# Weights as differences of suffix products, and a softmax divided at the gates

## The chip, the cores and the metric

One Trainium2 chip, one of its cores. The metric is the device time of one execution of the whole program, in microseconds (us). A core has five engines with queues of their own, which run in order: PE (matmul and transposes), DVE (vector), ACT (activation functions and copies), POOL (general vector work) and SP, which here issues every DMA.

## The reference, cut to what matters

One layer is run on a prompt of 1024 tokens and on a sample of 32 tokens with caches of 512. From one input projection come queries, keys, values and gates for two groups of eight heads of width 64. The A heads are a softmax over a band of 64-token chunks with a bias by clipped distance. The B heads are stick-breaking attention: a key's weight is its own sigmoid times the product of the complements of all later keys. Both outputs are multiplied with a SiLU of their gates.

```python
def band_attention(q, k, v, q_pos, k_pos, bias_table):
    s = jnp.einsum('bqhd,bkhd->bhqk', q, k).astype(jnp.float32) * ATTN_SCALE
    rel = jnp.clip(k_pos[None, :] - q_pos[:, None], -REL_CLIP, REL_CLIP) + REL_CLIP
    s = s + bias_table[:, rel].astype(jnp.float32)[None]
    ...
    w = jax.nn.softmax(s, axis=-1).astype(v.dtype)
    return jnp.einsum('bhqk,bkhd->bqhd', w, v)

def stick_breaking(q, k, v, q_pos, k_pos):
    z = jnp.einsum('bqhd,bkhd->bhqk', q, k).astype(jnp.float32) * ATTN_SCALE
    causal = (k_pos[None, :] < q_pos[:, None])[None, None]
    log_beta = jax.nn.log_sigmoid(z)
    log_1m = jnp.where(causal, jax.nn.log_sigmoid(-z), 0.0)
    after = lax.cumsum(log_1m, axis=3, reverse=True) - log_1m
    w = jnp.where(causal, jnp.exp(log_beta + after), 0.0).astype(v.dtype)
    return jnp.einsum('bhqk,bkhd->bqhd', w, v)

def finish(h, oa, ga, ob, gb, w_out, g_post, p, w_ple, w_ple_gate):
    y = jnp.concatenate([oa * jax.nn.silu(ga), ob * jax.nn.silu(gb)], axis=-1) @ w_out
    h = h + rmsnorm(y, g_post)
    return h + jax.nn.sigmoid(h @ w_ple_gate) * (p @ w_ple)
```

## The kernel before, in words

**Who sets the order.** The program is not issued as it is written. Every operation is recorded (`Recorder.add`) with its engine, its operands and what it must follow. `Recorder.order` then runs a list scheduling over all recorded operations, with a cost for each form (`Recorder.cost`), 60 ns per semaphore, 400 ns of margin ahead of PE and 2 us behind a DMA. On PE, class 0 (attention) goes ahead of class 1 (projections) whenever both are ready. `emit` issues the result, so nearly all instructions carry its line, L450, and are told apart by their tiles. The order on each engine is fixed by then; on the chip an engine only waits.

**Numbers.** Matmuls split an operand into a rounded high part and a rest (`kdA` and `klA`, `wTh` and `wTl`, `hnh` and `hnl`), so a product takes two or three matmuls.

**The stages.** After an opening (norm of the input, first projections, part of the per-layer embedding), eight pairs of heads follow in the order A0, B0, A1, B1 up to A3, B3. While the heads of one pair are computed, `weave` lays in the projections `q`, `k`, `v` of the next (`col_steps`, tiles `mm_qA` and so on, 3 chunks of 352 columns, 24 matmuls each). With the last pair, B3, come the eight gate projections, `gA` of four pairs and then `gB`. The two output products follow, as a seven-product scheme over four row blocks (`o0P` to `g3P`), and a tail.

**One head** (`attention`) has eight row blocks of 128 queries. `scores` computes a block: two matmuls for a piece of up to 512 keys into a PSUM bank of tag `S` (three of them). Blocks of more than 512 keys are done as two pieces. Working tiles come from two rings, `om` (w0) and `be` (w1, 3384 columns).

- *A* adds the bias and takes the running maximum in one DVE operation (`om<-SA,biasA`, tile `statA` for the maximum); DVE negates the maximum, ACT takes the exponential with the sum of the row, DVE the reciprocal, and POOL scales the block:

```python
                nc.vector.tensor_scalar(m[:, 2:3], m[:, last:last + 1], -1.0, None, ALU.mult)
                nc.scalar.activation(w1[:, 0:n], w0[:, 0:n], AF.Exp, bias=m[:, 2:3], accum_out=m[:, 3:4])
                nc.vector.reciprocal(m[:, 3:4], m[:, 3:4])
                nc.gpsimd.tensor_scalar(w1[:, 0:n], w1[:, 0:n], m[:, 3:4], 1.0, ALU.mult, ALU.mult)
```

- *B* adds a mask on the diagonal (DVE), takes sigmoid(-z) into w0 and sigmoid(z) into w1 (ACT), runs a product from the last key backwards over w0, shifted by one slot (DVE scan, with a column of ones that POOL sets at the end), and POOL multiplies w1 with it.

`weights_t` turns a block: PE transposes four 128x128 squares into a bank of tag `T` (two of them, `ptwA`, `ptwB`), ACT copies it to `wTh`, DVE subtracts to get `wTl`. Blocks 4 and 6 of A go by a transpose on DVE and a swap through DRAM instead. `values` multiplies with the values (`PVA`, `PVB`), and the head's output goes to DRAM (`o_dr`).

**At the gates** (`mms` in `col_steps`, `k == "g"`) ACT takes the sigmoid of a chunk (`sggA`, three buffers), DVE multiplies it with the chunk, which frees the PSUM bank, POOL multiplies with the head outputs loaded back from `o_dr` (`oggA`, tag `bias`, two buffers), and the result goes to `og_dr`, from where the output products read it.

**The sample's heads** (`sample_attention`) come beside pairs A1, B1, A3 and B3 and divide their own softmax. Their output fills columns 1024 to 1055 of `o_dr`. The tag `stg` (three buffers) holds the projected `st` tiles of q, k and v, and after the gates the split inputs of the per-layer embedding (`php`) and rows of the output products.

Of the kernel before, what the change touches and what calls it, by code (L numbers as in the profile page):

```python
# [455 lines left out]
def stream_step(  # L456
# [19 lines left out]
    def scratch(shape, name):  # L476
        return Buf(shape, F32, name=name, real=dram.tile(shape, F32, tag=name, name=name))

    o_dr = [scratch([P, T], f"o_dr{n}") for n in range(8)]
    og_dr = scratch([8, P, T], "og_dr")  # L480
    h1_dr = scratch([T, D], "h1_dr")
    sum_dr = {w: scratch([4, 4, P, 512], f"sum_dr{w}") for w in "og"}
# [28 lines left out]
    at0 = rec.pool(ctx, tc, name="at0", bufs=1)  # L511
    at = rec.pool(at_stack, tc, name="at", bufs=1)
    opnd = [at0, at]
    ring0, ring1 = Arena(rec, at, "om", 3076), Arena(rec, at, "be", 3384)
    ringh, ringl = (Arena(rec, at, x, 33 * P, F32R) for x in ("wTh", "wTl"))

    def rstd_of(ms, name, n):
# [6 lines left out]


    NAMES = ["qA", "kA", "vA", "gA", "qB", "kB", "vB", "gB"]

    raws, loaded = {}, {}

# [76 lines left out]
    def bias_rows():  # L606

        rb = ring0.tile([8, 257], "rb")
        dma(rb, rel_bias[0])
        R = ring1.tile([8, 768], "R")  # L610
        nc.gpsimd.memset(R, 0.0)
        nc.vector.tensor_scalar(R[:, 256:768], R[:, 256:768], rb[:, 0:1], None, ALU.add)
        nc.vector.tensor_copy(R[:, 0:256], rb[:, 0:256][:, ::-1])
        dma(r_dr, R)

    def bias_src(h, rows, first, cols):
# [95 lines left out]
    def col_steps(j):  # L712

        kind, p = order[j]
        ab, k = kind[1], kind[0]
        n = sidx(ab, p)
        box = {}
        steps = []

        def mms(c, part):  # L720
            if part == 0:
                if c == 0:
                    ensure(j)
                    ensure(j + 1)
                    if k != "g":
                        box["st"] = at2.tile([P, T], F32, tag="stg", name=f"st{kind}{p}", bufs=3)
                box["acc"] = psum("mm", f"mm_{kind}{p}_{c}")[:, 0:CH]
            acc = box["acc"]
            cs = slice(c * CH, (c + 1) * CH)
            if k == "g" and part == 0:  # L730
                box["og"] = at2.tile([P, CH], F32, tag="bias", name=f"og{kind}{p}_{c}", bufs=2)
                dma(box["og"], o_dr[n][:, cs])
            W = loaded[j]
            for x in range(part * 24 // PARTS, (part + 1) * 24 // PARTS):
                q, k8 = x // KD, x % KD
                a = W[k8 // 4][1 if q == 1 else 0]
                b = (hnl if q == 2 else hnh)[c]
                nc.tensor.matmul(acc, a[:, k8 % 4, :], b[:, k8, :], start=(x == 0), stop=(x == 23))
            if part < PARTS - 1:
                return  # L740
            if k == "g":
                sg = at2.tile([P, 512], F32, tag="sg", name=f"sg{kind}{p}_{c}", bufs=3)[:, 0:CH]
                nc.scalar.activation(sg, acc, AF.Sigmoid)
                nc.vector.tensor_tensor(sg, acc, sg, ALU.mult)
                nc.gpsimd.tensor_tensor(sg, sg, box["og"], ALU.mult)
                dma(og_dr[n, :, cs], sg)
            elif k == "q":
                nc.scalar.activation(box["st"][:, cs], acc, AF.Copy, scale=SCALE)
            else:
                nc.scalar.copy(box["st"][:, cs], acc)  # L750

        for c in range(NCH):
            for part in range(PARTS):
                steps.append((3.6 / PARTS, lambda c=c, part=part: mms(c, part), GATE_NEEDS.get((kind, p)) if part == 0 else None))

        def after_q():
            src_of["q", ab, p] = box["st"]
            nc.gpsimd.tensor_scalar(qsS[:, slot(ab, p), :], box["st"][:, SEQ:T], 1.0, 1.0, ALU.mult, ALU.mult)

        def after_k():  # L760
            src_of["k", ab, p] = box["st"]
            nc.gpsimd.tensor_scalar(ksS[:, slot(ab, p), :], box["st"][:, SEQ:T], 1.0, 1.0, ALU.mult, ALU.mult)

        def after_v(tok):
            src_of["v", ab, p] = tok
            dma(vs_dr[ab][:, p * P:(p + 1) * P], tok[0:NS, 8, :])

        if k == "q":
            steps.append((0.0, after_q))
        elif k == "k":  # L770
            steps.append((0.0, after_k))
            steps += keys_out(ab, p, lambda: box["st"], *((ak_p, ak_s) if ab == "A" else (bk_p, bk_s)))
        elif k == "v":
            steps += values_out(ab, p, lambda: box["st"], *((av_p, av_s) if ab == "A" else (bv_p, bv_s)), after_v)
        return steps


    def attention(ab, p, h):
# [5 lines left out]
        def begin():  # L784
            if ab == "A":
                bias = at2.tile([P, 640], F32, tag="bias", name=f"bias{nm}", bufs=2)
                dma(bias, bias_src(2 * p + h, P, 0, 640))
                nc.gpsimd.memset(bias[0:HD, 0:HD], NEG)
                nc.gpsimd.memset(bias[HD:P, 576:640], NEG)
                box["bias"] = bias  # L790

        def lo_block(i):
            return max(0, i - 4) if ab == "A" else 0
# [19 lines left out]
        def scores(i):  # L813
            L, kd, kl = Lq[h], KDh[h], KLD[h]
            b0 = lo_block(i)
            n = (i + 1 - b0) * P
            k0 = b0 * P
            cut = [0, n] if n <= 512 else [0, n // 2, n]
            w0, w1 = rooms(i)
            pieces = []  # L820
            for j in range(len(cut) - 1):
                s = psum("S", f"S{nm}_{i}_{j}")[:, 0:cut[j + 1] - cut[j]]
                lhs = L[:, i * P:(i + 1) * P]
                ks = slice(k0 + cut[j], k0 + cut[j + 1])
                nc.tensor.matmul(s, lhs, kd[:, ks], start=True, stop=False)
                nc.tensor.matmul(s, lhs, kl[:, ks], start=False, stop=True)
                pieces.append((cut[j], cut[j + 1], s))
            if ab == "B":
                a, b, s = pieces[-1]
                dg = s[:, b - a - P:b - a]  # L830
                nc.vector.tensor_tensor(dg, dg, maskb, ALU.add)
                nc.gpsimd.memset(w0[:, n:n + 1], 1.0)
                for a, b, s in pieces:
                    nc.scalar.activation(w0[:, a:b], s, AF.Sigmoid, scale=-1.0)
                for a, b, s in pieces:
                    nc.scalar.activation(w1[:, a:b], s, AF.Sigmoid)
                for a, b, s in reversed(pieces):
                    rev = w0[:, a + 1:b + 1][:, ::-1]
                    nc.vector.tensor_tensor_scan(rev, rev, s, 1.0 if b == n else w0[:, b + 1:b + 2], ALU.mult, ALU.bypass)
                nc.gpsimd.tensor_tensor(w1[:, 0:n], w1[:, 0:n], w0[:, 1:n + 1], ALU.mult)  # L840
            else:
                m = small.tile([P, 4], F32, tag="stat", name=f"stat{nm}_{i}", bufs=6)
                for j, (a, b, s) in enumerate(pieces):
                    nc.vector.tensor_tensor_reduce(
                        w0[:, a:b], s, box["bias"][:, n - b:n - a][:, ::-1], 1.0,
                        -3e38 if j == 0 else m[:, j - 1:j], ALU.add, ALU.max, m[:, j:j + 1])
                last = len(pieces) - 1
                nc.vector.tensor_scalar(m[:, 2:3], m[:, last:last + 1], -1.0, None, ALU.mult)
                nc.scalar.activation(w1[:, 0:n], w0[:, 0:n], AF.Exp, bias=m[:, 2:3], accum_out=m[:, 3:4])
                nc.vector.reciprocal(m[:, 3:4], m[:, 3:4])  # L850
                nc.gpsimd.tensor_scalar(w1[:, 0:n], w1[:, 0:n], m[:, 3:4], 1.0, ALU.mult, ALU.mult)
            state[i] = w0, w1

        wT = {}
# [92 lines left out]
    def sample_attention(ab, gi):  # L947
# [44 lines left out]
        def scores():  # L992
# [20 lines left out]
            else:  # L1013
                m = small.tile([P, 4], F32, tag="stat", name="stat" + nm, bufs=6)
                for j, (a0, b0, s) in enumerate(pieces):
                    nc.vector.tensor_tensor_reduce(
                        w0[:, a0:b0], s, bx["bias"][:, NK - b0:NK - a0][:, ::-1], 1.0,
                        -3e38 if j == 0 else m[:, 0:1], ALU.add, ALU.max, m[:, j:j + 1])
                nc.vector.tensor_scalar(m[:, 2:3], m[:, 1:2], -1.0, None, ALU.mult)
                nc.scalar.activation(w1[:, 0:NK], w0[:, 0:NK], AF.Exp, bias=m[:, 2:3], accum_out=m[:, 3:4])  # L1020
# [360 lines left out]
    for x in ple.later:  # L1381
        dma(*x)
        rec.behind()
    bias_rows()
    for h in range(4):
        dma(masks[h * NS:(h + 1) * NS, :], maskb[0:NS, 0:NS])
    for j in range(3):
# [463 lines left out]
```

## Time and profile before

| | us |
|---|---|
| median of 3 runs | 806.25 (804.82 to 810.35) |
| span of the profiled execution | 802.6 |
| PE busy | 792.0 |
| DVE, ACT, POOL busy | 565.7, 539.5, 469.5 |
| mean granted TensorE clock | 0.999 |

The profile is one execution, from its first to its last instruction, 802.6 us; the runs' times are 2.2 to 7.8 us longer than that span. A group of the profile has its engine, operation, tiles and shapes; then the time in which at least one of its instructions ran and the mean ns of one (instructions overlap, so the mean times the count can be more), then the engine's idle time ahead of them and what ended it. In a timeline, a row has its start, the time until its end, and how many instructions it merges; the difference of two starts on PE is the step at which instructions follow each other. A wait is put down to the engine whose signal came last.

### The profile page before, as it was taken

Reading aid. Unit: us, or ns where it says so; the run is one execution under the profiler, and the core shown is the slowest. Engines: PE = TensorE matmul, PEld = TensorE weight load, DVE = VectorE, ACT = ScalarE, POOL = GpSimd, SP = SyncE. Lnnn points to the kernel's source line nnn. Section 1 sums busy time; section 2 is a strip of 40 time slices with the busy share of each in tenths; the row PEclk is TensorE's granted clock in tenths of the full one; section 3 lists DMA queues with packets and bytes.
Section 4 is the critical chain, followed back from the end, with each engine's and each line's share of the span. In section 5 each row is a group of like instructions: output and inputs, shape, how many; then the busy total and the mean of one; then the engine's idle time right before and its main releaser. Section 6 shows DMA issues by size and latency. Waiting matters only on the chain.

```text
span 802.6 us, 14554 instructions
## 1 busy us (share of the span) xinstructions
PE 792.0 (99%) x4734; PEld 731.4 (91%) x4734; DVE 565.7 (70%) x1129; ACT 539.5 (67%) x1163; POOL 469.5 (58%) x554
## 2 busy tenths in 40 slices
PE   9999999999999999999999999999999999999997
PEld 7899999999999999999999899999998877888786
DVE  7627878777787888776787586854554786587655
ACT  6636787786586777776787577644437868876741
POOL 6625867795686866635473265554553448599613
PEclk9999999999999999999999999999999999999999
DMA  9419986538876565833325656344389957769634
GB/s 293 135 46 285 236 230 186 153 112 254 220 229 198 145 184 158 208 103 102 92 60 141 146 158 205 99 149 138 105 277 300 288 174 242 236 197 345 215 117 131
DMA packets 147390, 146.32 MB, mean 182 GB/s; under 512 B 37409, under 2 KB 109257, under 8 KB 147314
## 3 DMA queue, kind: packets, MB, share of 16 engines
q1 hardware_dynamic: 147314, 145.39, 61.3%
q8 instruction: 38, 0.62, 0.3%
q14 instruction: 38, 0.31, 0.1%
HBM read 90.78 MB, written 46.16 MB: 171 GB/s over the span
## 4 chain that ended last, share of the span: by engine, by line
PE 89%; DVE 3%; DMA 2%; POOL 2%; ACT 1%; issue 1%; SPq 1%; POOLq 0%; DVEq 0%; ACTq 0%
PE mm_gB L450 6%; PE mm_gA L450 6%; PE mm_kB L450 6%; PE mm_qB L450 6%; PE mm_qA L450 5%; PE mm_kA L450 5%; PE mm_vB L450 4%; PE PVB L450 4%; PE mm_vA L450 4%; PE SB L450 4%; PE ptwB L450 4%; PE SA L450 3%; PE PVA L450 3%; PE g0P L450 2%; PE g1P L450 2%; PE o1P L450 2%
## 5 line engine op out<-in xcount | busy, mean ns | idle before, releaser
L450 POOL TENSOR_TENSOR be<-be,om 128x512 f32<-128x512 f32 (+8 forms) x66 | 82.9, 1260 | 77.8 <-DVE om L450 43.9
L450 DVE TENSOR_TENSOR_SCAN om<-om,SB 128x384 f32<-128x384 f32 (+5 forms) x96 | 92.6, 968 | 21.9 <-ACT be L450 11.7
L450 POOL TENSOR_SCALAR be<-be,statA 128x640 f32<-128x640 f32 (+3 forms) x64 | 44.4, 698 | 44.4 <-DVE statA L450 35.8
L450 DVE TENSOR_TENSOR wTl<-ptwB,wTh 128x512 fp32r<-128x512 f32 (+3 forms) x96 | 50.8, 546 | 13.8 <-ACT wTh L450 12.4
L450 ACT ACTIVATE om<-SB 128x384 f32<-128x384 f32 (+5 forms) x96 | 47.4, 499 | 19.0 <-DVE SB L450 14.2
L450 ACT CAST wTh<-ptwB 128x512 fp32r<-128x512 f32 (+3 forms) x96 | 44.6, 483 | 14.5 <-PE ptwB L450 10.5
L450 ACT ACTIVATE be<-om,statA 128x640 f32<-128x640 f32 (+3 forms) x64 | 44.6, 698 | 11.2 <-DVE statA L450 9.6
L450 ACT ACTIVATE be<-SB 128x384 f32<-128x384 f32 (+5 forms) x96 | 46.8, 498 | 6.8 <-DVE om L450 6.3
L450 PE MATMUL ptwB<-ident,be 128*128 128x128 f32 x288 | 44.0, 273 | 0.1
L450 PEld LDWEIGHTS ptwB<-ident,be 128*128 128x128 f32 x288 | 34.9, 140 | 2.2 <-PE mm_vA L450 0.4
L450 DVE CUSTOM_DVE_ANT_0 om<-SA,biasA 128x320 f32<-128x320 f32 (+2 forms) x64 | 30.7, 480 | 5.3 <-PE SA L450 4.9
L450 PE MATMUL SB<-kdB,LB 128*128 128x384 f32 (+5 forms) x96 | 34.0, 357 | 0.3 <-DVE om L450 0.3
L450 ACT CAST wTh<-ptwA 128x512 fp32r<-128x512 f32 (+2 forms) x64 | 26.0, 429 | 12.0 <-PE ptwA L450 11.4
L450 DVE TENSOR_TENSOR wTl<-ptwA,wTh 128x512 fp32r<-128x512 f32 (+2 forms) x64 | 29.7, 482 | 4.9 <-ACT wTh L450 4.0
L450 PE MATMUL SB<-klB,LB 128*128 128x384 f32 (+5 forms) x96 | 32.9, 347 | 0.0
L450 PE MATMUL SA<-kdA,LA 128*128 128x320 f32 (+2 forms) x96 | 30.0, 319 | 1.1 <-DVE LA L450 0.8
L450 PE MATMUL SA<-klA,LA 128*128 128x320 f32 (+2 forms) x96 | 29.8, 319 | 0.0
L450 POOL TENSOR_TENSOR gB<-gB,gB 128x256 f32<-128x256 f32 x32 | 26.6, 848 | 0.7 <-DMA gB<-in_w_ple_gate_dram 0.4
L450 PE MATMUL ptwA<-ident,be 128*128 128x128 f32 x160 | 26.5, 274 | 0.0
L450 DVE TENSOR_TENSOR SB<-SB,maskb 128x128 f32<-128x128 f32 x64 | 18.0, 292 | 9.9 <-PE SB L450 8.0
L450 POOL TENSOR_TENSOR oB<-oB,oB 128x256 f32<-128x256 f32 x32 | 23.6, 754 | 1.4 <-DMA oB<-in_w_out_dram 1.3
L450 POOL TENSOR_TENSOR h<-h,x 128x512 f32<-128x512 f32 (+1 forms) x18 | 23.0, 1295 | 0.8 <-DVE h L450 0.8
(706 smaller groups left out, 2668.3 us busy)
## 6 DMA issues: line engine op xcount, KB each, us to landing
swapA<-om SPq DMA_DIRECT2D x16, 320.0 KB, 3.5
be<-swapA SPq DMA_DIRECT2D x64, 80.0 KB, 2.9
oB<-in_w_out_dram SPq DMA_DIRECT2D x16, 256.0 KB, 3.9
sum_dro<-oB SPq DMA_DIRECT2D x16, 256.0 KB, 2.9
gB<-in_w_ple_gate_dram SPq DMA_DIRECT2D x16, 256.0 KB, 3.7
sum_drg<-gB SPq DMA_DIRECT2D x16, 256.0 KB, 3.2
x<-in_x_prompt_dram SPq DMA_DIRECT2D x16, 256.0 KB, 4.1
h_dr<-h SPq DMA_DIRECT2D x8, 512.0 KB, 3.6
```

The costliest lines, as they stand in the source:

```text
L450: getattr(getattr(tc.nc, o.what[0]), o.what[1])(*args, **kw)
```

## The change

*B.* The second sigmoid goes. The scan runs over w0 in place and unshifted, from the column of ones at its end, so that w0 holds the products of the complements from each key on; a weight is the difference of two neighbours, which POOL takes in place of its product.

*A.* Queries are scaled by -1/8 and the bias rows are negated, so the DVE operation takes a minimum of the negated scores, and ACT's exponential (scale -1) uses it directly as its bias. Weights are left undivided. The row sums of a head's eight blocks gather in one 128x8 tile (`sums`); after the eighth, DVE takes reciprocals, PE turns them (`pts`), ACT copies them out and a DMA stores eight rows of 128 in `rs_dr` in DRAM. At the gates of A, two DMAs per chunk spread the rows of the two heads over 64 partitions each, and POOL multiplies once more. Columns of the sample in `rs_dr` are ones. The loaded tiles at the gates have two halves and come from tag `stg`. Ring `be` has 3328 columns.

```diff
-    ring0, ring1 = Arena(rec, at, "om", 3076), Arena(rec, at, "be", 3384)
+    ring0, ring1 = Arena(rec, at, "om", 3076), Arena(rec, at, "be", 3328)
...
+    def fixed_columns():
+        x = small.tile([8, NS], F32, tag="fixed", name="fixed")
+        nc.gpsimd.memset(x, 1.0)
+        dma(rs_dr[:, SEQ:T], x)
...
-        nc.vector.tensor_scalar(R[:, 256:768], R[:, 256:768], rb[:, 0:1], None, ALU.add)
-        nc.vector.tensor_copy(R[:, 0:256], rb[:, 0:256][:, ::-1])
+        nc.vector.tensor_scalar(R[:, 256:768], R[:, 256:768], rb[:, 0:1], None, ALU.subtract)
+        nc.vector.tensor_scalar(R[:, 0:256], rb[:, 0:256][:, ::-1], -1.0, None, ALU.mult)
...
-                box["og"] = at2.tile([P, CH], F32, tag="bias", name=f"og{kind}{p}_{c}", bufs=2)
-                dma(box["og"], o_dr[n][:, cs])
+                box["og"] = at2.tile([P, 2, CH], F32, tag="stg", name=f"og{kind}{p}_{c}", bufs=3)
+                dma(box["og"][:, 0], o_dr[n][:, cs])
+                if ab == "A":
+                    for h in range(2):
+                        row = rs_dr.real[2 * p + h:2 * p + h + 1, cs]
+                        dma(box["og"][h * HD:(h + 1) * HD, 1], Raw(rs_dr, bass.AP(tensor=row.tensor, offset=row.offset, ap=[[0, HD], [1, CH]])))
...
-                nc.gpsimd.tensor_tensor(sg, sg, box["og"], ALU.mult)
+                nc.gpsimd.tensor_tensor(sg, sg, box["og"][:, 0], ALU.mult)
+                if ab == "A":
+                    nc.gpsimd.tensor_tensor(sg, sg, box["og"][:, 1], ALU.mult)
...
-                nc.scalar.activation(box["st"][:, cs], acc, AF.Copy, scale=SCALE)
+                nc.scalar.activation(box["st"][:, cs], acc, AF.Copy, scale=-SCALE if ab == "A" else SCALE)
...
-                for a, b, s in pieces:
-                    nc.scalar.activation(w1[:, a:b], s, AF.Sigmoid)
                 for a, b, s in reversed(pieces):
-                    rev = w0[:, a + 1:b + 1][:, ::-1]
-                    nc.vector.tensor_tensor_scan(rev, rev, s, 1.0 if b == n else w0[:, b + 1:b + 2], ALU.mult, ALU.bypass)
-                nc.gpsimd.tensor_tensor(w1[:, 0:n], w1[:, 0:n], w0[:, 1:n + 1], ALU.mult)
+                    rev = w0[:, a:b][:, ::-1]
+                    nc.vector.tensor_tensor_scan(rev, rev, s, w0[:, b:b + 1], ALU.mult, ALU.bypass)
+                nc.gpsimd.tensor_tensor(w1[:, 0:n], w0[:, 1:n + 1], w0[:, 0:n], ALU.subtract)
...
-                        -3e38 if j == 0 else m[:, j - 1:j], ALU.add, ALU.max, m[:, j:j + 1])
+                        3e38 if j == 0 else m[:, j - 1:j], ALU.add, ALU.min, m[:, j:j + 1])
                 last = len(pieces) - 1
-                nc.vector.tensor_scalar(m[:, 2:3], m[:, last:last + 1], -1.0, None, ALU.mult)
-                nc.scalar.activation(w1[:, 0:n], w0[:, 0:n], AF.Exp, bias=m[:, 2:3], accum_out=m[:, 3:4])
-                nc.vector.reciprocal(m[:, 3:4], m[:, 3:4])
-                nc.gpsimd.tensor_scalar(w1[:, 0:n], w1[:, 0:n], m[:, 3:4], 1.0, ALU.mult, ALU.mult)
+                nc.scalar.activation(w1[:, 0:n], w0[:, 0:n], AF.Exp, bias=m[:, last:last + 1], scale=-1.0, accum_out=sums[:, i:i + 1])
+                if i == 7:
+                    nc.vector.reciprocal(sums, sums)
+                    pt = psum("T", f"pts{nm}")
+                    nc.tensor.transpose(pt[0:8, 0:P], sums, ident)
+                    row = at.tile([P, 4 * P], F32, tag="ot", name=f"sumrow{nm}", bufs=2)[0:8, 0:P]
+                    nc.scalar.copy(row, pt[0:8, 0:P])
+                    dma(rs_dr[2 * p + h, 0:SEQ].rearrange("(i q) -> i q", q=P), row)
```

The sample's A heads change only by the sign: minimum for maximum, and no negation. In the bias tiles the masked corners become +1e30.

More of the change, by code (lines that the diff above doesn't have):

```diff
@@ L479, in stream_step @@
     o_dr = [scratch([P, T], f"o_dr{n}") for n in range(8)]
+    rs_dr = scratch([8, T], "rs_dr")
     og_dr = scratch([8, P, T], "og_dr")
@@ L787, in begin @@
                 dma(bias, bias_src(2 * p + h, P, 0, 640))
-                nc.gpsimd.memset(bias[0:HD, 0:HD], NEG)
-                nc.gpsimd.memset(bias[HD:P, 576:640], NEG)
+                nc.gpsimd.memset(bias[0:HD, 0:HD], -NEG)
+                nc.gpsimd.memset(bias[HD:P, 576:640], -NEG)
                 box["bias"] = bias
+                box["sums"] = small.tile([P, 8], F32, tag="sums", name=f"sums{nm}", bufs=2)
         def lo_block(i):
@@ L834, in scores @@
                     nc.scalar.activation(w0[:, a:b], s, AF.Sigmoid, scale=-1.0)
-                for a, b, s in pieces:
-                    nc.scalar.activation(w1[:, a:b], s, AF.Sigmoid)
                 for a, b, s in reversed(pieces):
-                    rev = w0[:, a + 1:b + 1][:, ::-1]
-                    nc.vector.tensor_tensor_scan(rev, rev, s, 1.0 if b == n else w0[:, b + 1:b + 2], ALU.mult, ALU.bypass)
-                nc.gpsimd.tensor_tensor(w1[:, 0:n], w1[:, 0:n], w0[:, 1:n + 1], ALU.mult)
+                    rev = w0[:, a:b][:, ::-1]
+                    nc.vector.tensor_tensor_scan(rev, rev, s, w0[:, b:b + 1], ALU.mult, ALU.bypass)
+                nc.gpsimd.tensor_tensor(w1[:, 0:n], w0[:, 1:n + 1], w0[:, 0:n], ALU.subtract)
             else:
                 m = small.tile([P, 4], F32, tag="stat", name=f"stat{nm}_{i}", bufs=6)
+                sums = box["sums"]
                 for j, (a, b, s) in enumerate(pieces):
@@ L1017, in scores @@
                         w0[:, a0:b0], s, bx["bias"][:, NK - b0:NK - a0][:, ::-1], 1.0,
-                        -3e38 if j == 0 else m[:, 0:1], ALU.add, ALU.max, m[:, j:j + 1])
-                nc.vector.tensor_scalar(m[:, 2:3], m[:, 1:2], -1.0, None, ALU.mult)
-                nc.scalar.activation(w1[:, 0:NK], w0[:, 0:NK], AF.Exp, bias=m[:, 2:3], accum_out=m[:, 3:4])
+                        3e38 if j == 0 else m[:, 0:1], ALU.add, ALU.min, m[:, j:j + 1])
+                nc.scalar.activation(w1[:, 0:NK], w0[:, 0:NK], AF.Exp, bias=m[:, 1:2], scale=-1.0, accum_out=m[:, 3:4])
                 nc.vector.reciprocal(m[:, 3:4], m[:, 3:4])
@@ L1384, in stream_step @@
     bias_rows()
+    fixed_columns()
     for h in range(4):
```

## The prediction

> **What bounds the kernel now.** I read the page's busy times first, then a table of stages, then who made PE wait, then single stretches of PE's timeline. The page, with its span and its engines:
>
> ```profile
> span 802.6 us, 14554 instructions
> PE 792.0 (99%) x4734; PEld 731.4 (91%) x4734; DVE 565.7 (70%) x1129; ACT 539.5 (67%) x1163; POOL 469.5 (58%) x554
> ```
>
> PE is busy for 792.0 of 802.6 us. The other engines have room on average, but an average hides stages, so the next view cuts the span into the opening, the attention heads, the gates with the last head, the two final products and the tail. Its columns are PE, weight loads, DVE, ACT, POOL, granted clock, DMA share and GB/s.
>
> ```profile
> 0.00:40.00 40.00, 36.97 (x210) 32.79 (x211) 28.38 (x44) 25.26 (x49) 24.51 (x46) 1.00 0.68 215
> 40.00:480.00 440.00, 437.59 (x2840) 422.44 (x2839) 330.94 (x751) 314.28 (x695) 266.03 (x332) 1.00 0.60 166
> 480.00:600.00 120.00, 120.00 (x773) 117.61 (x772) 73.55 (x124) 63.33 (x145) 66.61 (x70) 1.00 0.52 160
> 600.00:780.00 180.00, 180.00 (x831) 144.01 (x830) 121.74 (x193) 132.79 (x268) 105.86 (x102) 1.00 0.73 238
> 780.00:802.60 22.60, 17.49 (x88) 14.56 (x86) 11.14 (x19) 3.79 (x7) 6.45 (x5) 0.98 0.36 117
> ```
>
> PE's idle time is 3.03 us in the opening, 5.11 us in the tail, and 440 - 437.59 = 2.41 us in all the attention between them; the gates and the products have none. The change touches neither opening nor tail in any step that sets their length. So 2.41 us is what can be won as idle time. The view of waits, PE alone, from 40 to 780 us, names most of it:
>
> ```profile
> PE SA L450 <- DVE LA L450: 0.8, 1, 0.8
> PE mm_vB L450 <- ACT wh_vB L450: 0.4, 1, 0.4
> PE SB L450 <- DVE om L450: 0.3, 1, 0.3
> PE PVA L450 <- ACT wTh L450: 0.2, 1, 0.2
> PE SA L450 <- DVE statA L450: 0.2, 1, 0.2
> ```
>
> The first of these, 0.8 us, is the first head's queries being split, which stays as it is. So 1.6 us can be won at most.
>
> Busy is not the same as fast, so I compare PE's step in the middle of attention (first two rows) with its step where nothing but gate matmuls runs (last two):
>
> ```profile
> 302.20 1.46 PE L450 MATMUL mm_kB<-hnh,wh_kB 128*128 128x352 f32 x8
> 303.50 0.32 PE L450 MATMUL mm_kB<-hnh,wl_kB 128*128 128x352 f32 x1
> ...
> 587.32 1.46 PE L450 MATMUL mm_gB<-hnh,wl_gB 128*128 128x352 f32 x8
> 588.61 1.45 PE L450 MATMUL mm_gB<-hnl,wh_gB 128*128 128x352 f32 x8
> ```
>
> Eight matmuls take 303.50 - 302.20 = 1.30 us in the one place and 1.29 us in the other, 0.162 us each. There is no hidden waiting inside the busy time of attention.
>
> **What the change removes.** These groups shrink or go:
>
> ```profile
> L450 POOL TENSOR_TENSOR be<-be,om 128x512 f32<-128x512 f32 (+8 forms) x66 | 82.9, 1260 | 77.8 <-DVE om L450 43.9 <-ACT be L450 12.3 <-ACT wTh L450 10.6
> L450 POOL TENSOR_SCALAR be<-be,statA 128x640 f32<-128x640 f32 (+3 forms) x64 | 44.4, 698 | 44.4 <-DVE statA L450 35.8 <-issue 3.8 <-PE mm_vA L450 1.8
> L450 ACT ACTIVATE be<-SB 128x384 f32<-128x384 f32 (+5 forms) x96 | 46.8, 498 | 6.8 <-DVE om L450 6.3 <-DVE wTl L450 0.6
> L450 DVE RECIPROCAL statA<-statA 128x1 f32<-128x1 f32 x64 | 9.7, 155 | 3.8 <-ACT be L450 3.3
> L450 DVE TENSOR_SCALAR statA<-statA 128x1 f32<-128x1 f32 x64 | 9.5, 149 | 1.2
> ```
>
> B loses its second sigmoid, 96 x 0.498 us, 46.8 us of ACT. Its POOL product becomes a POOL difference of two stretches of one tile: two inputs and one output of the same length, so I keep 1.26 us each. A loses 64 negations (9.5 us of DVE), 64 reciprocals less the 8 wider new ones (about 8.5 us), and 64 POOL scalings, 44.4 us. None of this is PE's, and PE is what fills the stage: the removed 109 us lie beside 437.59 busy us of PE. On PE's own time they are worth nothing beyond the 1.6 us of waits above.
>
> The scan of B now starts from the slot that POOL fills with 1.0. That is no new wait: the old scan already ran over that slot, and the trace shows it waiting there:
>
> ```profile
> L450 DVE TENSOR_TENSOR_SCAN om<-om,SB 128x256 f32<-128x256 f32 x8 | 5.4, 681 | 1.3 <-POOL om L450 0.7 <-ACT be L450 0.3 <-ACT om L450 0.3
> ```
>
> **What it adds on PE.** Each of the 8 A heads gets one transpose of its 128x8 sums. Transposes of the trace, as a group and as a run of seven:
>
> ```profile
> L450 PE MATMUL ptwB<-ident,be 128*128 128x128 f32 x288 | 44.0, 273 | 0.1
> 300.47 0.93 PE L450 MATMUL ptwB<-ident,be 128*128 128x128 f32 x7
> 301.15 1.22 PE L450 MATMUL mm_vA<-hnl,wh_vA 128*128 128x352 f32 x6
> ```
>
> 44.0/288 is 0.153 us; the run gives (301.15 - 300.47)/7 = 0.097 us. Eight cost 0.8 to 1.2 us; I take **+1.0 us**, because each stands alone between matmuls. [...]
>
> The transpose waits for the reciprocal of all eight sums, and PE's whole list stands behind it. The last link of that chain:
>
> ```profile
> L450 ACT ACTIVATE be<-om,statA 128x640 f32<-128x640 f32 (+3 forms) x64 | 44.6, 698 | 11.2 <-DVE statA L450 9.6 <-DVE wTl L450 0.6 <-POOL wl_vB L450 0.5
> ```
>
> In PE's new list it comes at the closest 4.1 us of matmuls after the head's last scores. Two exponentials and a reciprocal, 2 x 0.70 + 0.16 us, fit into that, so I charge no wait; if they did not fit, one exponential per head would cost 8 x 0.70 = 5.6 us.
>
> **What it adds beside PE.** The gates of A get a second POOL product and two row loads per chunk:
>
> ```profile
> L450 POOL TENSOR_TENSOR sggA<-sggA,oggA 128x352 f32<-128x352 f32 x12 | 11.5, 960 | 11.0 <-DVE sggA L450 9.7 <-issue 1.3
> oggA<-o_dr SPq DMA_DIRECT2D x12, 176.0 KB, 3.0
> 576.32 29.26 PE mm_gB L450 x181
> 606.01 6.07 PE ple L450 x26
> ```
>
> Twelve more products are 11.5 us of POOL in a stage where POOL is busy 66.61 of 120 us. Their cover is PE: a chunk is 24 x 0.162 = 3.9 us of matmuls, against 2 x 0.96 us. With 8 row stores, 24 row loads and one store of ones, SP issues 33 more DMAs. A row load waits for the last A head's row; behind it on SP stand gate weights and stores of gates. A gate's bank is freed by DVE's product, before POOL, and three buffers hold the gates, so PE would wait only if POOL fell three chunks, 11.7 us, behind. If that cover were gone, each late chunk would cost up to 0.96 us.
>
> The loaded tile moves to the tag `stg`. The first input tile of the per-layer embedding (`php`) then waits until the third-last gate is multiplied. The chain shows those products only after the last gate matmul, at 606.01; two more chunks, 7.8 us, stand between, so this costs nothing; uncovered it would be about one gate's product, 0.96 us. Behind that waiting copy stand, on ACT, the sigmoids of the last two gates.
>
> **What moves.** All engines' orders are worked out anew, so I compared PE's two lists, counting steps of the trace. From a block's last score matmul to its first weight transpose PE now has a median of 14.6 us of other work for A (12.5 before) and 16.7 us for B (13.7 before): the chain is shorter and gets more time. Against that, the PSUM banks turn more tightly. A bank of transposes comes back after one copy and one subtraction:
>
> ```profile
> L450 ACT CAST wTh<-ptwB 128x512 fp32r<-128x512 f32 (+3 forms) x96 | 44.6, 483 | 14.5 <-PE ptwB L450 10.5 <-PE PVB L450 3.0
> L450 DVE TENSOR_TENSOR wTl<-ptwB,wTh 128x512 fp32r<-128x512 f32 (+3 forms) x96 | 50.8, 546 | 13.8 <-ACT wTh L450 12.4 <-PE PVB L450 0.6
> ```
>
> That is 1.03 us. Returns in which PE's list leaves under 1.5 us rise from 4 to 14 for these banks and from 8 to 13 for the score banks, 12 to 27 in all. The waits above that are returns of score banks (behind `om` and `statA`) are 0.5 us; in proportion that makes 1.1. I take **+0.6 us**; nothing if the freed DVE and ACT return banks sooner, +2.0 us if all 1.6 us grow in that proportion.
>
> ACT's list holds ten table loads instead of eight; the two new ones stand where the last A head meets the last B head, as one B sigmoid is drawn ahead of three A exponentials.
>
> ```profile
> L450 ACT ACT_TABLE_LOAD x8 | 10.3, 1283 | 0.8 <-PEq L1839 0.7
> 301.81 1.28 ACT L450 ACT_TABLE_LOAD   x1
> 456.43 0.33 PE L450 MATMUL PVA<-wTh,v2A 128*128 128x128 f32 x1 [0.25 <-ACT wTh L450]
> 461.02 1.24 PE L450 MATMUL mm_vB<-hnh,wh_vB 128*128 128x352 f32 x6 [0.38 <-ACT wh_vB L450]
> ```
>
> Two are 2.6 us of ACT. The load at 301.81 lies beside PE rows without a gap (above), while at 456 to 461 us PE did wait 0.63 us for ACT. So 0 to 2.6 us; I take **+0.6 us**, that same wait once more. [...]
>
> **The sum.** 802.6 + 1.0 + 0.6 + 0.6 = 804.8 us of span. The median of the runs shown, 806.25 us, lies 3.65 us above this span; the runs lie between 804.82 and 810.35. So I forecast **808.5 us**, 0.3% above before. A change under 1%, about 8 us, is about what a measurement of this kernel cannot tell from none.
>
> **Rivals.**
> - *Relief (chance 0.22).* All 1.6 us of waits go, no new ones come, and only the transposes stay: 0.8 - 1.6, about 805.4 us. The longer median distances speak for it, the tighter bank returns against it.
> - *Slower through the transposes' banks (0.11).* In the 27 tight returns a scan or a mask addition comes between ACT's copy and DVE's subtraction. If each falls short by 0.4 us, that is 10.8 us: 817 to 819 us. It decides from 0.3 us each. Against it: twelve such returns now show 0.5 us in all.
> - *Hidden slack (0.04).* [...] As a mechanism here: weight loads fill 422.44 of 440 us; if the other 17.6 us were matmuls held up by late data, and half came back, the time would be about 798 us. The equal steps of 1.30 and 1.29 us speak against it.
> - *The gates do not hide their extra work (0.03).* 12 late chunks at 0.96 us and the sum above: about 820 us. The 120.00 busy us of 120 speak against.
>
> The forecast itself gets 0.60. Relief and forecast are both within 1%; 0.03 of hidden slack passes -1%, and 0.13 of the two slow cases passes +1%. That makes faster 0.03, same 0.84, slower 0.13. The range goes from relief less the runs' own lower scatter (805.4 - 2.4) to the terms at their upper ends, 1.2 + 2.0 + 2.6 = 5.8 us, with 2 us for the runs: **803 to 814 us**.
>
> **What would show it.** Right: PE busy near 793 us; ACT near 497 us, POOL near 437 us; PE idle from 40 to 480 us between 2 and 5 us, with waits for `wTl`, `om` or table loads near 450 us; none in the gates. A median distance that pays would show as fewer than 1.6 us of waits. Wrong: PE idle over 8 us in attention, PE waiting for `sggA` or `php` near 600 us, or PE's step in attention changing from 0.162 us.

## The result and the profile after

The changed kernel took 813.21 us (median of 12 runs, 808.41 to 816.58), the kernel before 806.27 us (12 runs, 804.82 to 811.13). The ratio is 1.0067, 95% interval 1.0047 to 1.0088: slower by two thirds of a per cent, inside the predicted range, 4.7 us above the predicted time. The profiled execution of after took 814.83 us, its span is 812.0 us, 9.4 us longer than that of before. First the page of after, span and engines:

```profile
span 812.0 us, 14302 instructions
PE 794.0 (98%) x4742; PEld 732.1 (90%) x4742; DVE 565.6 (70%) x1007; ACT 507.3 (62%) x1077; POOL 432.7 (53%) x503
```

ACT lost 32 us and POOL 37 us of work, and PE, which sets the time, is as busy as it was (792.0 before). The span grew by idle PE. The table of stages (stretch, its length, then PE, weight loads, DVE, ACT, POOL, granted clock, DMA share, GB/s) says where:

```profile
0.00:40.00 40.00, 35.61 (x205) 31.22 (x206) 27.56 (x43) 24.99 (x49) 24.32 (x47) 1.00 0.65 214
40.00:480.00 440.00, 434.05 (x2817) 418.23 (x2816) 321.08 (x627) 287.82 (x627) 217.12 (x267) 1.00 0.60 165
480.00:600.00 120.00, 120.00 (x775) 117.62 (x775) 72.67 (x121) 54.52 (x123) 77.52 (x82) 1.00 0.58 172
600.00:780.00 180.00, 177.50 (x824) 142.87 (x823) 128.11 (x193) 132.71 (x269) 105.98 (x102) 0.99 0.73 236
```

Idle PE is 4.39 us in the opening (3.03 before), 5.95 us in attention (2.41), nothing in the gates, and 2.50 us in the two final products, which had none. The view of waits, PE alone, 40 to 780 us (who waited for whom; total, times, longest):

```profile
PE g0P L450 <- DVE uu L450: 2.5, 1, 2.5
PE ptwA L450 <- ACT be L450: 1.1, 1, 1.1
PE SB L450 <- DVE om L450: 0.9, 3, 0.4
PE SsA L450 <- ACT QsA L450: 0.8, 1, 0.8
PE SA L450 <- DVE LA L450: 0.7, 1, 0.7
PE PVA L450 <- ACT wTh L450: 0.6, 1, 0.6
PE SA L450 <- DVE statA L450: 0.6, 1, 0.6
PE PVA L450 <- DVE sumsA L450: 0.4, 1, 0.4
PE SA L450 <- DVE statsA L450: 0.3, 1, 0.3
```

The first is in the last product, far from anything that the change edits. The timeline there, POOL, DVE and PE of after (start, length, engine, instructions; in brackets the idle time before):

```profile
732.82 2.54 POOL L450 TENSOR_TENSOR ug<-ug,s 128x512 f32<-128x512 f32 x2
735.32 1.29 POOL L450 TENSOR_TENSOR gT<-raw,gT 128x512 fp32r<-128x512 f32 x1
...
739.08 2.54 POOL L450 TENSOR_TENSOR gB<-raw,gB 128x512 fp32r<-128x512 f32 x2
734.13 8.03 DVE L450 TENSOR_TENSOR gT<-raw,gT 128x512 fp32r<-128x512 f32 x1
741.39 0.40 PE L450 MATMUL g1P<-gT,wlA22g 128*128 128x512 f32 x1
744.29 3.79 PE L450 MATMUL g0P<-gT,S1g 128*128 128x512 f32 x10 [2.50 <-DVE uu L450]
747.88 1.43 PE L450 MATMUL pth<-ident,ht 128*128 128x128 f32 x8
749.07 0.71 PE L450 MATMUL g0P<-gT,S1g 128*128 128x512 f32 x2
```

One subtraction on DVE, both of whose operands lie in SBUF, takes 8.03 us; the same one takes 1.79 us in before. POOL runs from before its start to 741.62 without a gap, so five POOL operations begin while the subtraction waits, and it ends 0.54 us after the last of them. DVE's queue is then late with `uu`, and PE waits 2.50 us. A second loss follows: from the first row of `g0P` to its second, 744.29 to 749.07, PE needs 4.78 us, where in before it needed 3.09 for the same instructions:

```profile
736.39 2.46 PE L450 MATMUL g0P<-gT,S1g 128*128 128x512 f32 x10
738.69 1.03 PE L450 MATMUL pth<-ident,ht 128*128 128x128 f32 x8
739.48 0.71 PE L450 MATMUL g0P<-gT,S1g 128*128 128x512 f32 x2
```

The table of two-microsecond stretches of after shows what goes with it, a granted clock of one half behind the wait:

```profile
746.00:748.00 2.00, 2.00 (x6) 1.41 (x6) 1.32 (x3) 0.67 (x2) 1.17 (x1) 0.50 0.76 271
```

So this one event cost 2.50 + 1.69 = 4.2 us of the 9.4. Two theories were to be tested. **P**: the subtraction is held by the POOL operations beside it, because both of its operands lie in SBUF; whether that happens is a matter of chance in each execution, not of the change. **O**: the newly worked-out order of all engines makes the rest, in attention, by table loads, tight bank returns or steps planned too close.

### The profile page after: what moved, and what is told of

The parts are those of the page before. It is cut to its first block, busy times and chain, and to the rows that moved or that the text cites. A ratio compares the mean times of both kernels' runs of the same rounds, so it can differ in the third digit from the quotient of the medians.

```text
span 812.0 us, 14302 instructions
## 1 busy us (share of the span) xinstructions
PE 794.0 (98%) x4742; PEld 732.1 (90%) x4742; DVE 565.6 (70%) x1007; ACT 507.3 (62%) x1077; POOL 432.7 (53%) x503
## 4 chain that ended last, share of the span: by engine, by line
PE 82%; POOL 6%; DMA 4%; ACT 3%; DVE 2%; issue 1%; SPq 1%; POOLq 0%; ACTq 0%; DVEq 0%
PE mm_gB L450 6%; PE mm_gA L450 6%; PE mm_qA L450 5%; PE mm_kA L450 5%; PE mm_vA L450 5%; PE mm_kB L450 5%; PE mm_qB L450 4%; PE PVB L450 4%; PE mm_vB L450 4%; PE ptwB L450 4%; PE SB L450 4%; PE PVA L450 3%; PE SA L450 3%; PE o1P L450 2%; PE g2P L450 2%; PE o0P L450 2%
## 5 line engine op out<-in xcount | busy, mean ns | idle before, releaser
L450 POOL TENSOR_TENSOR be<-om 128x128 f32<-128x128 f32 (+7 forms) x64 | 74.9, 1175 | 71.1 <-DVE om L450 51.4
L450 DVE TENSOR_TENSOR_SCAN om<-om,SB 128x384 f32<-128x384 f32 (+5 forms) x96 | 95.8, 1007 | 17.5 <-ACT om L450 15.5
L450 ACT ACTIVATE om<-SB 128x384 f32<-128x384 f32 (+5 forms) x96 | 44.8, 492 | 34.6 <-DVE SB L450 23.2
L450 POOL TENSOR_TENSOR sggA<-sggA,oggA 128x352 f32<-128x352 f32 x24 | 23.9, 997 | 10.5 <-DVE sggA L450 9.5
L450 POOL TENSOR_TENSOR klA<-stkA,kdA 64x1024 fp32r<-64x1024 f32 x8 | 20.2, 2526 | 8.9 <-ACT kdA L450 8.5
L450 POOL TENSOR_TENSOR sggB<-sggB,oggB 128x352 f32<-128x352 f32 x12 | 13.3, 1105 | 20.4 <-DVE sggB L450 13.1
```

The lines of the kernel that those rows point to most:

```text
L450: getattr(getattr(tc.nc, o.what[0]), o.what[1])(*args, **kw)
```

## Experiments

**The changed kernel once more, unchanged (e4).**

> The changed kernel as it is, a second profiled execution. Theory P: if the subtraction gT on DVE is held behind POOL in every execution, its row is again about 8 us long and PE waits 2.5 us for uu near 744; if it is a matter of timing, it is 0.7 to 2 us long and the span is about 808 us. Theory O: the waits at the ends of A heads (PE behind wTh, QsA, statA, om, be; 3.5 us more than before in all) come at the same places again, whatever the last product does. Time 811 to 814.

Measured: 810.58 us (808.58 to 813.36, 12 runs). The runs fall into two groups, six from 808.58 to 809.38 and six from 811.78 to 813.36. The profiled one belongs to the lower group, span 806.6 us, and there the held subtraction and POOL's operation behind it read, in the timelines of this run:

```profile
733.12 1.79 DVE L450 TENSOR_TENSOR gT<-raw,gT 128x512 fp32r<-128x512 f32 x1
734.31 1.76 POOL L450 TENSOR_TENSOR gT<-raw,gT 128x512 fp32r<-128x512 f32 x1
```

Here DVE got in at POOL's next boundary, and POOL paid 0.47 us for it. Of the first 12 runs of after, 11 lie at 811.69 us or more. So the same program takes either course, 17 times of 24 the long one. The phase does not tell the two courses apart: taking two merged POOL operations as equal steps, an estimate from their rows, the subtraction starts 0.06 us behind the start of a POOL operation in after, in e4 and in before. PE's waits in attention came at the same places with nearly the same lengths: those belong to the order.

**One operand of the subtraction in PSUM, in after (e5) and in before (e8).** The expectations call this "off the port". The port is a name for what DVE and POOL contend for; no run shows what that is, only what it does to the times.

```
-            split_slice(b, kt, raw, nc.scalar, nc.vector if count[0] % 3 == 0 else nc.gpsimd)
+            if off and count[0] % 3 == 0:          # off: last product only
+                beside = psum("mm", f"rawps{count[0]}")
+                nc.scalar.copy(beside, raw)
+                nc.scalar.copy(b[:, 0, kt, :], raw)
+                nc.vector.tensor_tensor(b[:, 1, kt, :], beside, f(b[:, 0, kt, :]), ALU.subtract)
+            else:
...
```

> The changed kernel, with the DVE splits of the last product reading a copy that ACT puts into a PSUM bank, so that only one operand of theirs lies in SBUF. PE's order up to that stage is the same. Theory P: no DVE row of over 2 us near 734, no 2.5 us wait for uu, the granted clock in 740 to 760 us back from 0.91 to near 1.0; the time falls by about 3.9 us to 809. Rival (DVE was late for another reason, such as its own queue or the banks): a wait of 2 us or more for DVE stays in 700 to 760 us, and the time stays at 812 to 814. If it happens only in some executions, the fall is smaller, 1 to 3 us, and the scatter shrinks.

> The kernel before with the last product's DVE splits off the port, as in e5. The runs of the kernel before fall into a larger group near 805.9 and some at 808.5 to 811 us. Theory P: the upper group is the same starvation, so it goes, the median stays at 805.5 to 806 and the scatter shrinks to about 1.5 us. Rival (the upper group has another cause, a clock that falls by itself): runs at 809 to 811 us come in the same share as before, about one in four.

Measured: after 808.59 us (808.09 to 809.65), ratio to before 1.0025, interval 1.0012 to 1.0037; before 806.29 us (805.40 to 807.33), ratio 0.9977, interval 0.9960 to 0.9994. The upper groups are gone in all 24 runs. The kernel before had one too: 28 of its 70 runs beside these experiments lie above 808 us, though no kept profile is of one of them. Theory P holds in what it says of the time. The median of e8 is that of before; what it gains is the upper group. The edit does more than move an operand: it orders that stage anew, and POOL's run in e5 has a pause of 1.64 us from 734.07 on. So it does not show by itself which of the two frees DVE. The subtraction at 733.77 in e5 does start in the middle of a POOL operation (732.76, 1.31 us long) and takes 0.68 us, which speaks for the operand. The change itself, freed of the event, costs 808.59 - 806.29 = 2.3 us. These two medians come from two sets of runs, in which the runs of before under 808 us have medians of 806.01 and 806.10.

**What holds the subtraction (e10, e13).** Neither kernel computes anything of the task: POOL additions or subtractions back to back, and one DVE operation with two SBUF operands started among them.

> Nothing of the task is computed: each section starts n additions on POOL back to back (128x512, two SBUF operands, about 1.27 us each) and, during the first of them, one subtraction on DVE of the same shape. Its operands lie both in SBUF (two2 to two16; late8 to latest8 start it 0.6, 1.2 and 1.8 us later; gap8 and gap16 let POOL wait once in the middle for a copy on ACT) or one of them in PSUM (one8, one16). Theory P, held until POOL has a gap: the DVE row is about as long as what is left of POOL's run, some 1.3 us in two2, 4 in two4, 9 in two8 and 19 in two16, half of that in gap8 and gap16, and 0.7 us in one8 and one16. Rival (the two only take turns, instruction by instruction): two2 to two16 all take 1 to 2.5 us. A mixture, in which the phase decides, would show late8 to latest8 apart from two8.

Measured, in DVE's timeline of e10 (the second row is the section with 16 POOL operations, the third meets a POOL operation at its start, the last has one operand in PSUM):

```profile
12.61 0.68 DVE L44 TENSOR_TENSOR two<-go,x 128x512 f32<-128x512 f32 x1
36.41 1.25 DVE L44 TENSOR_TENSOR two<-go,x 128x512 f32<-128x512 f32 x1
57.95 1.75 DVE L44 TENSOR_TENSOR late<-go,x 128x512 f32<-128x512 f32 x1
134.43 0.68 DVE L44 TENSOR_TENSOR one<-bank,x 128x512 f32<-128x512 f32 x1
```

The contention is real: 0.68 us without POOL or with an operand in PSUM, 1.0 to 1.75 us with two SBUF operands beside POOL. But DVE waits here for one boundary and no more (1.25 us in the section with 16 POOL operations), so "held until POOL has a gap" does not hold here, and the rival, turns, fits these rows. Turns do not explain the 8.03 us, in which five POOL operations in a row began ahead of DVE. The next expectation counts six lost boundaries; the rows show five.

> Nothing of the task is computed: 288 sections, each with 6 subtractions on POOL back to back and one on DVE with two SBUF operands, which starts some 17 ns later from section to section, so that it meets POOL's run at every phase. Four passes of 72: plain float outputs; fp32r outputs as in the product's splits; the same with DMA loads running; the same with each POOL operation waiting for a copy of ACT that is long done. Left open by e10, where DVE got its turn at POOL's next boundary in all of its eight two-operand sections with a run behind them, at 1.0 to 1.75 us: what makes it lose six boundaries in the changed kernel (8.03 us). If it is the phase, one part of each pass has rows of 2.5 us or more and the rest stays at 1.9 us or less; if it is DMA traffic or waits on POOL, long rows stand in the third or fourth pass alone; if it is neither, all rows stay under 2 us and the cause of the lost boundaries stays open.

Measured, as groups of the four passes (72 operations each, busy us and mean ns), and the longest single row of the third:

```profile
L65 DVE TENSOR_TENSOR dvef<-go,x 128x512 f32<-128x512 f32 x72 | 89.0, 1236 | 0.0
L68 DVE TENSOR_TENSOR dvef32r<-go,x 128x512 fp32r<-128x512 f32 x72 | 90.2, 1253 | 0.0
L71 DVE TENSOR_TENSOR dvedma<-go,x 128x512 fp32r<-128x512 f32 x72 | 88.9, 1234 | 0.0
L74 DVE TENSOR_TENSOR dvewait<-go,x 128x512 fp32r<-128x512 f32 x72 | 87.9, 1221 | 0.0
1374.34 1.78 DVE L71 TENSOR_TENSOR dvedma<-go,x 128x512 fp32r<-128x512 f32 x1
```

No row of the 288 passes 1.78 us, at any phase that was met (none fell between 0.48 and 0.70 us into a POOL operation). The DMA loads did not run where they were meant to: they ran ahead and filled the first 553 us of the first pass (389 to 410 GB/s; the pass ends near 680 us), which therefore is the one that speaks for DMA. Phase, format, loads and waits that are long met do not, each alone, make DVE wait past POOL's next boundary. Why it waits past five in a row in the last product stays open.

**The two halves alone (e2: B's part on the kernel before; e3: A's part, the old B).**

```
-                for a, b, s in pieces:
-                    nc.scalar.activation(w1[:, a:b], s, AF.Sigmoid)
...
-                nc.gpsimd.tensor_tensor(w1[:, 0:n], w1[:, 0:n], w0[:, 1:n + 1], ALU.mult)
+                nc.gpsimd.tensor_tensor(w1[:, 0:n], w0[:, 1:n + 1], w0[:, 0:n], ALU.subtract)
```

> The kernel before with the B half of the change alone (one sigmoid, the scan in place, a difference on POOL); A stays. No new PE work. Theory O (the newly worked-out order with more table loads and tighter bank returns is what costs): ACT has 10 table loads instead of 8, 9 to 10 tight returns of either kind against 4 and 8; PE idle from 40 to 480 us rises from 2.4 to some 4 us, time about 808. Theory P (one DVE operation held behind POOL's unbroken run in the last product costs 3.9 us): no long gT subtraction here, since A's work is as before and the plan of the last product starts from another place; by P alone 806. Rival (relief: the 46.8 us off ACT pay): below 805.

> The changed kernel with the old B (two sigmoids, a product on POOL): the A half alone. It has the 8 transposes (1.0 us), the store of ones at the start and the extra work at the gates. Theory O: 14 table loads on ACT, each 1.3 us, and 10 and 12 tight returns; PE idle from 40 to 480 us 4 to 7 us, time 809 to 813. Theory P: 807.3 without a held DVE operation in the last product, about 811 with one. If A's rows and transposes themselves are the cost, the time is at the changed kernel's 813 and PE waits stand at the ends of A heads.

Measured: 813.15 us for B alone (ratio 1.0086, 1.0054 to 1.0118), 815.81 us for A alone (1.0108, 1.0083 to 1.0133). B alone adds nothing to PE, and I expected 808; for A alone I expected 809 to 813. Neither had a held subtraction in its profile (1.83 and 1.79 us), though some of their runs may have. Their largest waits, PE of e2 and of e3:

```profile
217.04 0.82 PE L450 MATMUL SsA<-Kh0sA,QsA 128*128 128x272 f32 x2 [2.74 <-ACT QsA L450]
481.25 1.12 PE L450 MATMUL ptwA<-ident,be 128*128 128x128 f32 x4 [3.89 <-ACT be L450]
```

Each half alone is slower than both together in the same set of runs (810.58 us, or 808.59 without the event). The halves don't add up, so the cost is no sum of what the instructions of each half cost. That it is the cost of the order which the planner makes of them is argued here, and tested below with other orders of the same work.

**The table loads (e6).** ACT's timeline of e5 at the last handover from A to B, with what PE waits for right behind:

```profile
469.62 1.28 ACT L450 ACT_TABLE_LOAD   x1
470.91 0.28 ACT L450 ACTIVATE om<-SB 128x128 f32<-128x128 f32 x1
471.08 0.58 ACT L450 CAST wTh<-ptwA 128x512 fp32r<-128x512 f32 x1
471.69 1.28 ACT L450 ACT_TABLE_LOAD   x1
472.98 0.83 ACT L450 ACTIVATE be<-om,statA 128x640 f32<-128x640 f32 x1
475.93 0.66 PE L450 MATMUL ptwA<-ident,be 128*128 128x128 f32 x4 [1.06 <-ACT be L450]
476.99 0.82 PE L450 MATMUL PVA<-wTh,v2A 128*128 128x512 f32 x4 [0.40 <-DVE sumsA L450]
479.12 0.41 PE L450 MATMUL SB<-kdB,LB 128*128 128x320 f32 x1 [0.25 <-DVE om L450]
```

One sigmoid is drawn ahead of the exponentials and brings two loads. To e5 I added a rule for the order:

```
...
+        for (k, x), (_, y) in zip(runs, runs[1:]):   # runs of Exp or Sigmoid, as written
+            for o in y:
+                o.after.update(x)
```

> The kernel e5 (changed kernel, last product's DVE splits off the port), with one rule more for the order: each run of exponentials or sigmoids, as written, waits for the whole run before it, so ACT's list holds 8 table loads again. PE's list is the same up to the last handover from A to B. Theory O, table loads: the waits at 475.9 (be, 1.06 us), 477.0 (sumsA, 0.40 us) and 479.1 us (om, 0.25 us) go, PE's idle time from 40 to 480 us falls from 5.9 to about 4.2 us, and the time falls by 1.7 us, to 806.9. Rival (bank returns or the longer chain of the sums make that wait): the waits stay within 0.3 us, and the time stays at 808.6.

Measured: 807.12 us (805.89 to 809.90), 1.5 us less than e5; ratio to before 0.9993 (0.9975 to 1.0011). Loads, and the attention rows of e6 and e8:

```profile
L460 ACT ACT_TABLE_LOAD x8 | 10.3, 1283 | 0.8 <-PEq L1871 0.7
40.00:480.00 440.00, 435.94 (x2831) 420.44 (x2830) 323.56 (x630) 287.72 (x629) 218.83 (x270) 1.00 0.60 165
40.00:480.00 440.00, 436.81 (x2830) 421.05 (x2829) 329.29 (x748) 312.54 (x691) 264.92 (x329) 1.00 0.60 165
```

The first two of the three waits are gone, the third is 0.18 us, and idle PE in attention is 4.06 us. What is left against e8 is 807.12 - 806.29 = 0.8 us by the runs, and 4.06 - 3.19 = 0.9 us by idle PE. A single profile can be off by as much: idle PE in attention is 2.41 us in before and 3.19 in e8, whose edit touches the last product alone.

**Other orders of the same work.** The planner adds a margin before PE may use a result; 0.4 us in both kernels. With e5's and e6's edits in both kernels, I raised it: e7 (after) and e9 (before) at 0.8 us, e11 (after) and e12 (before) at 0.5 us. At 0.4 us the row of before is e8, which lacks e6's rule; its list holds 8 table loads without it.

```
-MARGIN = 400
+MARGIN = 800
```

> e6 with the planner's margin for what PE waits for raised from 0.4 to 0.8 us. Returns of PSUM banks under 1.5 us fall from 27 (13 and 14) to 5 (2 and 3). Theory O, tight returns and steps planned too close: most of the remaining 4.2 us of PE's idle time in attention goes, to about 1.5 us, and the time is about 804 us, below the kernel before. Rival (a fresh order brings its own waits, whatever its margins): idle time stays at 4 us or more and the time at 807 or above.

> e8 with the rule for the table loads and the margin of 0.8 us: the kernel before in the order that e7 gives to the changed kernel. Tight returns 5 (1 and 4), 8 table loads. If the removed work has a value of its own once the order is dealt with, e7 is faster than this one; if the change is worth nothing beside PE, the two differ by the eight transposes alone, 0.8 to 1.2 us, in favour of this one. Time by the waits that stay: 804 to 806.

> e6 with the planner's margin at 0.5 instead of 0.4 us: a third order of the changed kernel's work (tight returns 12 and 9, 8 table loads). Theory O, put more widely: each newly worked-out order brings its own waits, worth more than the change; the time lies anywhere from 806 to 813, and its waits stand at other places than those of e6. Rival (the changed work has waits of its own): those behind QsA, statsA and statA at 214 to 219 us stay.

> e8 with the rule for the table loads and the margin of 0.5 us: the third order for the work of the kernel before (tight returns 5 and 4). Theory O, put more widely: its difference to e11 has no fixed sign or size (it was 0.8 us in favour of before at a margin of 0.4, 2.9 us in favour of after at 0.8); time 806 to 815. Rival (the change costs its transposes and no more): e12 is 0.8 to 1.2 us faster than e11.

| margin | after | before | after less before |
|---|---|---|---|
| 0.4 us | 807.12 (e6) | 806.29 (e8) | +0.8 |
| 0.5 us | 814.67 (e11) | 807.04 (e12) | +7.6 |
| 0.8 us | 811.96 (e7) | 814.81 (e9) | -2.9 |

The largest wait of PE in each of the four, e7, e9, e11, e12:

```profile
116.93 0.51 PE L460 MATMUL SB<-kdB,LB 128*128 128x512 f32 x1 [2.66 <-DVE om L460]
275.23 0.39 PE L460 MATMUL SsB<-Kh0sB,QsB 128*128 128x272 f32 x1 [1.68 <-ACT be L460]
219.59 0.52 PE L460 MATMUL SsA<-Kh0sA,QsA 128*128 128x272 f32 x2 [3.09 <-ACT QsA L460]
310.24 0.41 PE L460 MATMUL SA<-kdA,LA 128*128 128x320 f32 x1 [1.44 <-DVE statA L460]
```

My expectation for e7 failed: with 5 tight bank returns instead of 27 it is 4.8 us slower than e6. So a plan with fewer tight returns is not a faster one; e7's largest wait, 2.66 us, is for `om`, itself the return of a score bank. The times expected for e9 (804 to 806 us) and e11 (806 to 813) were too low as well. The three slow orders, e7, e9 and e11, have two or three waits of 1 to 3.1 us each, at other places in each; e12 has one, of 1.44 us, and e6 and e8 have none above 0.85 us behind the opening. The rival had one point: the wait behind `QsA` is in every order of after except e7, and in B alone, from 0.85 to 3.09 us. But the orders of one and the same work differ by 7.6 us (after) and 8.5 us (before), and the change's effect has both signs. Three orders are too few to say what the change is worth on average.

## Why the prediction was right, and where not

- *PE bounds, the removed work is worth nothing*: right. 32 and 37 us less of ACT and POOL moved the time nowhere. ACT was to be near 497 us and reads 507.3. Its groups sum to 45.1 us less, about what was predicted; the page's busy time counts overlapping records once, and sigmoids that overlapped their neighbours took only 32.2 us of it along.
- *No wait for the sums' chain*: nearly right. PE waits 0.40 us for `sumsA` in after, e4 and e5, behind the late exponentials, and 0.38 us for the copied sums (`sumrowA`) in e6.
- *Scan without a new wait, gates hidden, `php` free*: right. PE is busy 120.00 of 120 us at the gates, and no wait for `sggA` or `php` appears. The opening's 1.4 us are scatter of its loads (ACT waits 1.7 us there for a load of the input in after, 0.8 in before): PE is busy there for 35.61, 35.96, 35.94 and 36.92 us in after, e4, e5 and e6, the same work.
- *Transposes, +1.0 us on PE's busy time*: not seen. PE is busy 792.6 us with them (e6) and 792.5 us without (e8). If they cost, it is within the 0.8 us that stay between these two.
- *Table loads, +0.6 us*: the place and the mechanism were right, the size was not. Taking them away won 1.5 us, since behind the late exponentials stood PE's transposes, then the sums, then a score bank. The range of 0 to 2.6 us held it. A load showed no cost on ACT beyond its own 1.28 us: in e5 469.62 + 1.28 is 470.90, and the sigmoid starts at 470.91; the copy behind it ends at 471.66, and the next load starts at 471.69; in before 301.81 + 1.28 is 303.09, and the exponential starts at 303.10.
- *Tight bank returns, +0.6 us*: not confirmed. Returns and transposes together were to cost 1.6 us, and 0.8 to 0.9 us are left for both. e7 has fewer tight returns and more waits.
- *PE idle from 40 to 480 us, between 2 and 5 us*: missed. It is 5.95, 5.76 and 5.88 us in after, e4 and e5, below the 8 us that were to be a sign of being wrong. Of the 3.5 us over before, 1.7 stand at the last handover from A to B, behind the table loads. Another 1.8 stand at 214 to 220 us, where the first of the sample's A heads begins (`QsA` 0.85, `statsA` 0.34, `statA` 0.62); the prediction has no term for that place.
- *The sum without the event*: 1.0 + 0.6 + 0.6 = 2.2 us; measured 2.3 us (e5 against e8), and the forecast of 808.5 us is e5's 808.59. That they agree so closely is luck: the loads cost more than their term, returns and transposes less than theirs.
- *A change under 1% cannot be told from none*: not so here. The interval of 1.0047 to 1.0088 leaves out 1.
- *What was missing*: the products were read as 180.00 busy us of 180 and left out. The runs shown were 804.82, 806.25 and 810.35 us, and the third was a sign that this profile did not cover every course of the program. The event costs about 4 us. By the groups of times it struck after 17 times of 24 and before 28 times of 70. In the first 12 runs of after it struck 11 times, and that, not the change's own work, takes their median from some 808.5 to 813.2.

That the range held owes as much to its width, made for other costs, as to its working. Why after is struck more often than before was not settled; the share also differs between sets of runs of one kernel (11 of 12 and 6 of 12 for after; 5 of 23, 13 of 29 and 10 of 18 for before).

## What to carry to other kernels

Where one engine is full and a planner orders the rest, as here, an edit off that engine was priced by the waits of the new order, and those are read from the timeline of the changed order at each handover, table loads first (1.5 us here). Look at the scatter of the runs before trusting one profile: two groups of times were two courses of one program here, parted in the changed kernel by a DVE operation with two SBUF operands beside a long run of POOL (8.03 us in one profile, 1.79 us in the other). Putting one operand in PSUM, with the new order that came with it, took the upper group out of both kernels (no run above 809.65 us in after and 807.33 us in before). A change under 1% is compared in several orders of the same work before its sign is believed.

## What the hardware showed that was not expected

A long wait of PE cost more than its length, 4.2 us for 2.50 us in after. Behind each of six waits of 1.88, 2.50, 2.66, 2.74, 3.09 and 3.89 us (e11, after, e7, e2, e11, e3) a stretch of 2 us shows a granted clock of 0.50; behind waits of 1.06, 1.44, 1.60 and 1.68 us (e5, e12, e7, e9) it stays at 1.00. The stretches behind the one of 1.88 us (e11) and behind the one of 1.68 us (e9):

```profile
119.00:121.00 2.00, 2.00 (x9) 1.93 (x9) 2.00 (x4) 0.70 (x2) 0.98 (x2) 0.50 0.55 186
276.00:278.00 2.00, 1.87 (x13) 1.57 (x14) 2.00 (x4) 1.25 (x5) 2.00 (x2) 1.00 0.90 192
```

In after this added 1.69 us to a wait of 2.50. Read in slices of 0.2 us, each of the six falls lasts 3.4 us at one half, 1.7 us of lost clock, and begins 2.7 to 4.0 us after its wait began, in four of the six only when the matmuls run again. The length of the wait does not decide alone. At the end of the program PE has nothing left to do: e5's clock stays at 1.00 for the 5.0 us behind its last matmul, which ends at 801.77, while e8's falls 1.9 us behind its own, which ends at 799.45:

```profile
803.80:805.80 2.00, 0.00 (x0) 0.00 (x0) 0.10 (x1) 0.00 (x0) 0.00 (x0) 1.00 0.64 226
801.40:803.40 2.00, 0.00 (x0) 0.00 (x0) 0.18 (x1) 0.00 (x0) 0.00 (x0) 0.50 0.68 240
```

What else decides was not tested.
